# One hymba block on one core: borders of the first stage reordered, last chunk's q, k, v stores on GpSimd's queue, out-projection weights split in the first stage

## The chip, the cores and the metric

The kernel runs on 1 core of one Trainium2 chip. The metric is device time in microseconds (us) of one launch. TensorE is called PE here (its weight loads PEld), VectorE DVE, ScalarE ACT, GpSimd POOL or Pool, SyncE SP; those are the names that the profile uses.

## What is computed

One layer on a sequence of 2048 tokens of width 1024, fp32 in and out, cut to what matters here:

```
mod = silu(c) @ ada_w + ada_b                    # six vectors of 1024: shift, scale, gate, twice
h = rmsnorm(x) * (1 + scale1) + shift1
z = h @ w_in                                     # q, k, v (several branches), gates, zx, zy
o_nsa = compressed + selected + window attention, gated by sigmoid(zg)
   # compressed keys/values: gelu(blocks of 32 tokens @ cmp_w1) @ cmp_w2
o_lru = RG-LRU(zx) * gelu(zy)                    # conv of width 4, gates, a linear scan over the tokens
mixed = [rmsnorm(o_nsa) * nog, rmsnorm(o_lru) * log]
x = x + gate1 * (mixed @ w_out)
x = x + gate2 * conv_ffn(rmsnorm(x) * (1 + scale2) + shift2)
return rmsnorm(x) * final_norm_g
```

## The kernel before

Every matrix product that needs fp32 accuracy is three matmuls: both operands are split into a high part (`...h`, written by ACT as a copy in a shorter format) and a low part (`...l`, the difference, by DVE), and high x high, high x low and low x high are summed (L124, L125, `mm3` at L132).

The work has three stages, each with its tile pools. The first (0 to some 572 us of the trace) goes over four chunks of 512 tokens. A chunk is normalised (`norm_x`, L144 and L146: square, scale), transposed on PE and split (`norm_k`, L153 to L159: tiles `tp`, `hh`, `hl`), and then multiplied with tiles of 128 columns of `w_in`: `zc` (raw keys for compression, stored to C_d), `zx` (input of the RG-LRU), `zy`, `zq`, `zk`, `zv` with the gates. Weights come through `weights` in the order of the list `seq`: SP loads `wr`, ACT and DVE split it into `w..h`, `w..l`. q, k, v are split too and stored in DRAM (Q_d, K_d, V_d; buffers `st` x3 and `vst` x2). In the last chunk the compression's steps (`compress_load`, `compress_step`: load `xf` from C_d, split, multiply with `cmp_w1`) stand between the projections; the list TAIL gives the order of their weights.

Two side works run in the first stage. `ada_next` makes one more column block of `mod` at each call: SP loads `ad` (512 KB, one buffer: the next load waits until PE has used the one before), PE multiplies it (`aprb`, L174), and for the gate vectors SP also loads a row `ar` that DVE adds to and SP stores to G_d (L200 to L202). `wo_next` (chunks 1 and 2, in the loop over `zy`) multiplies 128 rows of `w_out` with the norms' gains and gate1 (DVE, L328) and stores the result to W_d as fp32.

The second stage ("t", attention, to about 1460 us) goes over 32 units of 128 tokens and one key group, beginning with tile 4: scores `sa` (compressed and window), minimum and exponential (`pc`), `ss` (selected blocks), transposed probabilities `pt` split into `th` (ACT) and `tl` (DVE), and `po`. `load_wo` (L630 to L637) loads W_d in this stage and splits it there into `wo`. The third stage is the FFN.

The order of instructions on each engine is not that of the code alone: a scheduler takes the code's order as a priority and each engine then runs its own list strictly in order, as does SP its DMA issues. So moving a call moves rows on all engines. What the change moves lies between about 40 and 700 us; from unit 4_1's successors on, and in the whole third stage, the order is as it was.

## Time and profile before

| | us |
|---|---|
| median of 3 runs | 2914.63 |
| lowest, highest | 2912.96, 2920.44 |
| profiled execution, its own time | 2917.85 |
| span in the trace (first to last instruction) | 2916.1 |

The profiled execution is 3.22 us above the median, and 1.75 us of it lie outside the span. Sums below are made against 2917.85 and then moved by -3.22 to the median. In the tables of stretches a line gives, for the stretch named first, its length and each engine's busy time with the number of instructions, then the mean granted clock of PE (1.00 is 2.4 GHz, 0.50 is 1.2 GHz), the share of the DMA engines and GB/s. In a timeline a line begins with its start and its duration; an idle time of the engine before it and what ended it stand in brackets.

### The profile page before, as it was taken

Reading aid. Unit: us, or ns where it says so; the run is one execution under the profiler, and the core shown is the slowest. Engines: PE = TensorE matmul, PEld = TensorE weight load, DVE = VectorE, ACT = ScalarE, POOL = GpSimd, SP = SyncE. Lnnn points to the kernel's source line nnn. Section 1 sums busy time; section 2 is a strip of 40 time slices with the busy share of each in tenths; the row PEclk is TensorE's granted clock in tenths of the full one; section 3 lists DMA queues with packets and bytes.
Section 4 is the critical chain, followed back from the end, with each engine's and each line's share of the span. In section 5 each row is a group of like instructions: output and inputs, shape, how many; then the busy total and the mean of one; then the engine's idle time right before and its main releaser. Section 6 shows DMA issues by size and latency. Waiting matters only on the chain.

```text
span 2916.1 us, 40471 instructions
## 1 busy us (share of the span) xinstructions
PE 2821.5 (97%) x14308; PEld 2324.5 (80%) x14308; DVE 1723.8 (59%) x3077; ACT 1484.6 (51%) x2686; POOL 1319.2 (45%) x1416
## 2 busy tenths in 40 slices
PE   8999999889999999999999999999999999999998
PEld 6777777767788777888788888888888888888887
DVE  4656656776777788888656621666216662266621
ACT  5656566577777677777643332433324333233322
POOL 1111010066666555555454445644455444555444
PEclk9999999989999999999999999999999999999999
DMA  7576765755544443443443333433334333343332
GB/s 287 178 271 201 244 210 141 208 162 138 145 124 127 121 128 104 115 120 105 153 139 94 100 118 101 152 96 100 122 97 152 99 94 123 101 138 94 97 99 80
DMA packets 262524, 399.47 MB, mean 137 GB/s; under 512 B 42033, under 2 KB 171057, under 8 KB 262321
## 3 DMA queue, kind: packets, MB, share of 16 engines
q1 hardware_dynamic: 261712, 395.70, 44.4%
q8 instruction: 114, 1.87, 0.3%
q0 software_dynamic: 320, 1.05, 0.1%
q14 instruction: 90, 0.73, 0.1%
q10 hardware_dynamic: 288, 0.13, 0.0%
HBM read 343.20 MB, written 53.61 MB: 136 GB/s over the span
## 4 chain that ended last, share of the span: by engine, by line
PE 80%; DVE 6%; ACT 5%; DMA 5%; issue 2%; POOL 1%; SPq 1%; POOLq 0%; DVEq 0%; ACTq 0%
PE pg L132 17%; PE pd L132 16%; PE pu L132 16%; PE p L132 6%; PE pt L786 5%; PE ss L647 3%; PE po L797 3%; PE po L798 3%; PE zy L132 2%; PE zx L132 2%; PE sa L647 2%; DMA xf<-C_d 1%; DVE tl L788 1%; PE zq L132 1%; ACT th L787 1%
## 5 line engine op out<-in xcount | busy, mean ns | idle before, releaser
L788 DVE TENSOR_TENSOR tl<-pt,th 128x512 fp32r<-128x512 f32 (+4 forms) x444 | 295.1, 683 | 47.6 <-ACT th L787 45.5
L945 DVE TENSOR_SCALAR ac<-gp,vec 128x512 f32<-128x512 f32 x88 | 191.5, 2176 | 201.5 <-ACT gp L942 198.8
L787 ACT ACTIVATE th<-pt 128x512 fp32r<-128x512 f32 (+4 forms) x444 | 254.7, 592 | 105.5 <-PE pt L786 100.8
L758 POOL TENSOR_SCALAR ps<-ps,rs,gates 128x1024 f32<-128x1024 f32 (+7 forms) x192 | 182.3, 959 | 163.2 <-DVE rs L755 118.8
L953 DVE TENSOR_TENSOR gl<-ac,gh 128x512 fp32r<-128x512 f32 x88 | 209.4, 2379 | 70.5 <-ACT gh L952 70.5
L978 DVE TENSOR_TENSOR y<-pd,g2b 128x512 f32<-128x512 f32 x32 | 21.9, 683 | 371.1 <-PE pd L132 371.1
L948 ACT ACTIVATE ac<-ac 128x512 f32<-128x512 f32 x88 | 55.6, 632 | 339.4 <-DVE ac L947 339.3
L752 ACT ACTIVATE ps<-ps,mn 128x1024 f32<-128x1024 f32 (+7 forms) x192 | 171.2, 895 | 52.3 <-DVE mn L652 51.9
L786 PE MATMUL pt<-ident,ps 128*128 128x128 f32 x1088 | 167.4, 275 | 6.0 <-DVE tl L788 5.2
L647 PE MATMUL ss<-ks,Q 128*128 128x512 f32 (+3 forms) x640 | 164.4, 379 | 4.2 <-DVE mn L652 2.9
L786 PEld LDWEIGHTS pt<-ident,ps 128*128 128x128 f32 x1088 | 133.1, 141 | 42.0 <-DVE tl L788 12.1
L647 PEld LDWEIGHTS ss<-ks,Q 128*128 128x128 f32 x640 | 116.2, 194 | 30.7 <-issue 4.8
L947 DVE SCALAR_TENSOR_TENSOR ac<-gp,vec,ac 128x512 f32<-128x512 f32 x176 | 134.3, 763 | 6.2
L798 PE MATMUL po<-tl,vs 128*128 128x512 f32 x272 | 123.6, 454 | 1.0 <-DVE tl L788 1.0
L797 PE MATMUL po<-th,vs 128*128 128x512 f32 x272 | 111.3, 409 | 6.4 <-ACT th L787 6.3
L652 DVE CUSTOM_DVE_ANT_1 ps<-ss,bi 128x1024 f32<-128x1024 f32 (+4 forms) x96 | 105.6, 1106 | 15.6 <-PE ss L647 10.3
L647 PE MATMUL sa<-K,Q 128*128 128x272 f32 (+14 forms) x464 | 99.1, 341 | 14.8 <-DVE mn L652 5.6
L786 PE MATMUL pt<-ident,pc 128*128 128x128 f32 (+9 forms) x688 | 103.7, 277 | 5.6 <-POOL pc L724 2.8
L726 POOL TENSOR_SCALAR pc<-pc,rs,gates 128x640 f32<-128x640 f32 (+4 forms) x128 | 104.2, 815 | 8.1 <-DVE mn L652 7.5
L401 POOL COPY hcar<-xc 128x1 f32<-128x1 f32 x16 | 19.4, 1212 | 180.7 <-DVE xc L400 180.0
L786 PEld LDWEIGHTS pt<-ident,pc 128*128 128x128 f32 (+9 forms) x688 | 81.7, 137 | 23.6 <-POOL pc L724 3.3
L949 DVE TENSOR_TENSOR ac<-ac,pu 128x512 f32<-128x512 f32 x88 | 60.5, 688 | 67.3 <-ACT ac L948 65.9
(1626 smaller groups left out, 8877.2 us busy)
## 6 DMA issues: line engine op xcount, KB each, us to landing
wg<-in_w_gu_dram SPq DMA_DIRECT2D x88, 512.0 KB, 3.6
wu<-in_w_gu_dram SPq DMA_DIRECT2D x88, 512.0 KB, 3.6
wd<-in_w_dn_dram SPq DMA_DIRECT2D x88, 512.0 KB, 3.6
wr<-in_w_in_dram SPq DMA_DIRECT2D x64, 512.0 KB, 5.5
ad<-in_ada_dram SPq DMA_DIRECT2D x32, 512.0 KB, 5.0
Q<-Q_d SPq DMA_DIRECT2D x64, 256.0 KB, 4.7
ks<-K_d SPq DMA_DIRECT2D x56, 256.0 KB, 3.4
vs<-V_d SPq DMA_DIRECT2D x56, 256.0 KB, 3.2
```

The costliest lines, as they stand in the source:

```text
L132: pe.matmul(ps, a, b, start=(n == 0), stop=(n == total - 1))
L647: pe.matmul(ps[:, o:o + W], Qt[:, hl, h * P:(h + 1) * P], K_ap, start=(hl == 0), stop=(hl == 1))
L752: act.activation(p, p, AF.Exp, scale=-1.0, bias=init, accum_out=sm[:, h, 2 + n:3 + n])
L758: pool.tensor_scalar(p, p, rs[:, h, 2:3], gt[:, h, 1:2], op0=OP.mult, op1=OP.mult)
L786: pe.transpose(pt[:, h * P:(h + 1) * P], jobs[n][0](h), ident)
L787: act.activation(th, pt, AF.Copy)
L788: dve.tensor_tensor(tl, pt, th.bitcast(F32), op=OP.subtract)
L797: pe.matmul(po, jobs[n][1], th, start=(n == 0), stop=False)
L798: pe.matmul(po, jobs[n][1], tl, start=False, stop=(n == N - 1))
L945: dve.tensor_scalar(ac, gp[:, 0:TC], V("fcw", f), V("fcb", f), op0=OP.mult, op1=OP.add)
L947: dve.scalar_tensor_tensor(ac, gp[:, k:k + TC], V("fcw", k * NF + f), ac, op0=OP.mult, op1=OP.add)
L953: dve.tensor_tensor(l, ac, h.bitcast(F32), op=OP.subtract)
```

## The change

- TAIL and `sequence`: in the last chunk the compression's steps and their weights begin after `zx3_1` and not after `zy3_0`; `compress_load(0)` comes right after `zc`. Then come the rest of q, then k, and v last.
- `norm_x` of the next chunk stands before the `zy` loop; it was before the q tiles.
- Two calls of `ada_next` move from the chunk's end to between q tiles. The sum of squares of the RG-LRU's output on PE (`pr`, L423) moves to the chunk's end (`lru_scale`).
- `wo_next` moves from the `zy` loop to the `zx` loop, takes its tiles from `st` instead of `x`, makes the split itself (ACT copy, DVE subtract) and stores both parts: W_d has twice the size. `load_wo` then loads 1 MB for each of 8 row blocks and splits nothing.
- In the last chunk all stores of q, k and v are issued from GpSimd's queue; before, only those of `qs3_3` were.

```diff
-TAIL = [("z", 4), ("c", 0), ("z", 5), ("c", 1), ("z", 6), ("c", 2), ("z", 7), ("c", 3), ("z", 8), ("c", 4), ("z", 9),
-        ("c", 5), ("z", 12), ("c", 6), ("z", 13), ("c", 7), ("v", 0), ("v", 1), ("z", 10), ("z", 11)]
+TAIL = [("z", 0), ("z", 1), ("c", 0), ("z", 2), ("c", 1), ("z", 3), ("c", 2), ("z", 4), ("c", 3), ("z", 5), ("c", 4),
+        ("z", 6), ("c", 5), ("z", 7), ("c", 6), ("z", 8), ("c", 7)] + [("z", j) for j in range(9, 14)] + [("v", 0), ("v", 1)]
...
-    W_d = dr.tile([KT, P, D], F32, name="W_d")
+    W_d = dr.tile([KT, P, 2, D], F32, name="W_d")
...
-            g1b = pl.tile([P, D], F32, name=f"g1b{k}", tag="x", bufs=4)
+            g1b = pl.tile([P, D], F32, name=f"g1b{k}", tag="st", bufs=3)
...
-            raw = pl.tile([P, D], F32, name=f"wor{k}", tag="x", bufs=4)
+            raw = pl.tile([P, D], F32, name=f"wor{k}", tag="st", bufs=3)
...
-            st = pl.tile([P, D], F32, name=f"wos{k}", tag="st", bufs=3)
-            dve.scalar_tensor_tensor(st, raw, gain, g1b, op0=OP.mult, op1=OP.mult)
-            sync.dma_start(W_d[k], st)
+            dve.scalar_tensor_tensor(raw, raw, gain, g1b, op0=OP.mult, op1=OP.mult)
+            h = pl.tile([P, D], F32R, name=f"wosh{k}", tag="st", bufs=3)
+            l = pl.tile([P, D], F32R, name=f"wosl{k}", tag="st", bufs=3)
+            act.activation(h, raw, AF.Copy)
+            dve.tensor_tensor(l, raw, h.bitcast(F32), op=OP.subtract)
+            sync.dma_start(W_d[k, :, 0, :], h.bitcast(F32))
+            sync.dma_start(W_d[k, :, 1, :], l.bitcast(F32))
...
+            if c + 1 == NCH:
+                compress_load(0)
...
                 ada_next()
-            if c + 1 == NCH:
-                compress_load(0)
+                if 0 < c < NCH - 1:
+                    wo_next()
+                if c + 1 == NCH and m > 0:
+                    compress_step(m - 1)
+            xs = norm_x(pl, x, c + 1, 4, ("t2", 2)) if c + 1 < NCH else None
             for m in range(4):
                 ps = z_tile(c, 4 + m, hT, f"zy{c}_{m}")
...
                 ada_next()
-                if 0 < c < NCH - 1:
-                    wo_next()
                 if c + 1 == NCH:
-                    compress_step(m)
+                    compress_step(m + 3)
...
+            def lru_scale():
                 pr = pp.tile([P, 4], F32, name=f"pr{c}", tag="g", bufs=2)
...
-                    (sync if c + 1 < NCH or j < 3 else pool).dma_start(
+                    (sync if c + 1 < NCH else pool).dma_start(
                         Q_d[h // 4, :, :, h % 4, t0:t0 + TC], st[hh * 64:(hh + 1) * 64].bitcast(F32))
...
-                    sync.dma_start(K_d[n, g, :, :, t0:t0 + TC].rearrange("l d t -> d l t"),
+                    (sync if c + 1 < NCH else pool).dma_start(K_d[n, g, :, :, t0:t0 + TC].rearrange("l d t -> d l t"),
...
-                    sync.dma_start(V_d[:, :, 4 * c + t].rearrange("n p g d -> p n (g d)"),
+                    (sync if c + 1 < NCH else pool).dma_start(V_d[:, :, 4 * c + t].rearrange("n p g d -> p n (g d)"),
...
             if c + 1 < NCH:
-                xs = norm_x(pl, x, c + 1, 4, ("t2", 2))
-                zs(range(8, 12))
+                zs((8, 9))
+                ada_next()
+                zs((10, 11))
+                ada_next()
                 lru_out()
...
                 v_tiles(lambda k: following(k + 3) if 1 <= k < 5 else None)
-                for _ in range(2):
-                    ada_next()
             else:
-                for n, j in enumerate((8, 9, 12, 13)):
-                    zs([j])
-                    compress_step(4 + n)
+                zs([8])
+                compress_step(7)
+                zs(range(9, 12))
                 lru_out()
+                zs((12, 13))
                 v_tiles()
-                zs((10, 11))
+            lru_scale()
             return nxt
...
-                raw = pl.tile([P, D], F32, name=f"wr{k}", tag="ps", bufs=10)
-                sync.dma_start(raw, W_d[k])
-                act.activation(t[:, 0], raw, AF.Copy)
-                dve.tensor_tensor(t[:, 1], raw, t[:, 0].bitcast(F32), op=OP.subtract)
+                sync.dma_start(t.bitcast(F32), W_d[k])
```

ACT at the start, where the last normalised parts of chunk 0 (`hh0_7`, `hl0_7`) are made, before:

```order
L176 ACTIVATE adrp7_573<-aprp7_556 128x256
L159 ACTIVATE hl0_6_536<-hf0_6_537,mod_78 128x512
L157 ACTIVATE hh0_7_585<-tp0_7_580,mod_78,A1_79 128x512
L176 ACTIVATE adrb16_683<-aprb16_674 128x128
L159 ACTIVATE hl0_7_586<-hf0_7_587,mod_78 128x512
L339 ACTIVATE cs0_0_647<-zf0_383 128x512
```

and in the changed kernel (`j1_..` and `x1_..` are the squares and scalings of chunk 1's tokens, `x1_0` to `x1_3`):

```order
L144 ACTIVATE j1_0_872,ss1_0_873<-x1_0_870 128x1024
L176 ACTIVATE adrp7_573<-aprp7_556 128x256
L144 ACTIVATE j1_1_881,ss1_1_882<-x1_1_879 128x1024
L159 ACTIVATE hl0_6_536<-hf0_6_537,mod_78 128x512
L146 ACTIVATE x1_0_870<-x1_0_870,rs1_0_875 128x1024
L144 ACTIVATE j1_2_890,ss1_2_891<-x1_2_888 128x1024
L157 ACTIVATE hh0_7_585<-tp0_7_580,mod_78,A1_79 128x512
L176 ACTIVATE adrb16_683<-aprb16_674 128x128
L146 ACTIVATE x1_1_879<-x1_1_879,rs1_1_884 128x1024
L144 ACTIVATE j1_3_899,ss1_3_900<-x1_3_897 128x1024
L146 ACTIVATE x1_2_888<-x1_2_888,rs1_2_893 128x1024
L159 ACTIVATE hl0_7_586<-hf0_7_587,mod_78 128x512
```

Both pieces begin behind `hh0_6`. Seven instructions of chunk 1's `norm_x` now stand between it and `hl0_7`.

SP at the border from chunk 2 to chunk 3 (`ad`: the next block of `ada_w`; `qs2_..`, `ls2_..`: stores of q and of the RG-LRU's output), before:

```order
L436 DMA Q_d_60<-qs2_1_3617 128x1x512 x2
L271 DMA wr54_3833<-in_w_in_dram 128x1024
L436 DMA Q_d_60<-qs2_2_3653 128x1x512 x2
L191 DMA ad42_3356<-in_ada_dram 128x1024
L202 DMA G2_d_82<-ar40_3313 128x128
L200 DMA ar41_3371<-in_rows_dram 128x128
L271 DMA wr55_3839<-in_w_in_dram 128x1024
L436 DMA Q_d_60<-qs2_3_3689 128x1x512 x2
L191 DMA ad43_3414<-in_ada_dram 128x1024
L417 DMA L_d_64<-ls2_0_3694 256x1x512
```

and in the changed kernel:

```order
L445 DMA Q_d_60<-qs2_1_3649 128x1x512 x2
L200 DMA ar41_3453<-in_rows_dram 128x128
L271 DMA wr54_3896<-in_w_in_dram 128x1024
L191 DMA ad43_3489<-in_ada_dram 128x1024
L445 DMA Q_d_60<-qs2_2_3704 128x1x512 x2
L202 DMA G2_d_82<-ar41_3453 128x128
L271 DMA wr55_3902<-in_w_in_dram 128x1024
L445 DMA Q_d_60<-qs2_3_3740 128x1x512
L200 DMA ar42_3504<-in_rows_dram 128x128
L445 DMA Q_d_60<-qs2_3_3740 128x1x512
L424 DMA L_d_64<-ls2_0_3764 256x1x512
```

`ad43` stands ahead of the stores of `qs2_2` and `qs2_3`; it stood behind them.

ACT at the end of the first stage (`vs3_..`: evacuation of v; `pc4_0`: the first exponentials of the attention stage), before:

```order
L463 ACTIVATE vs3_3_5301<-zv3_3_5189 128x4x64
L213 ACTIVATE get_5127<-get_5127 128x256
L432 ACTIVATE qs3_2_5331<-zq3_2_5306 128x512
L616 ACT_TABLE_LOAD
L616 ACTIVATE gates_86<-gates_86 128x384
L562 ACTIVATE VC_88<-vf_5139 128x2x64
L432 ACTIVATE qs3_3_5361<-zq3_3_5336 128x512
L699 ACT_TABLE_LOAD
L699 ACTIVATE pc4_0_5405,sm4_0_5407<-pc4_0_5405,mn4_0_5406 128x40
```

and in the changed kernel:

```order
L451 ACTIVATE ks3_0_5230<-zk3_0_5205 128x512
L572 ACTIVATE VC_88<-vf_5063 128x2x64
L451 ACTIVATE ks3_1_5266<-zk3_1_5241 128x512
L472 ACTIVATE vs3_0_5371<-zv3_0_5271 128x4x64
L472 ACTIVATE vs3_1_5376<-zv3_1_5272 128x4x64
L472 ACTIVATE vs3_2_5381<-zv3_2_5273 128x4x64
L472 ACTIVATE vs3_3_5386<-zv3_3_5274 128x4x64
L626 ACT_TABLE_LOAD
L626 ACTIVATE gates_86<-gates_86 128x384
L706 ACT_TABLE_LOAD
L706 ACTIVATE pc4_0_5437,sm4_0_5439<-pc4_0_5437,mn4_0_5438 128x40
```

The four `vs3` copies now stand directly ahead of the gates' sigmoid and the first exponentials, and the q copies ahead of them all. With two `vst` buffers `vs3_2` takes the buffer of `vs3_0`, whose store must have landed.

## Rows read from the trace of the kernel before

**Rows 1.** The page's first part: busy time, share of the span and instructions of each engine.

```profile
PE 2821.5 (97%) x14308; PEld 2324.5 (80%) x14308; DVE 1723.8 (59%) x3077; ACT 1484.6 (51%) x2686; POOL 1319.2 (45%) x1416
```

**Rows 2.** Table of stretches: three chunk borders, last chunk, start of attention, zx of chunk 1.

```profile
122.00:185.00 63.00, 55.19 (x371) 45.56 (x369) 32.95 (x52) 36.40 (x60) 9.21 (x13) 0.95 0.68 226
262.00:312.00 50.00, 45.50 (x325) 37.73 (x323) 25.63 (x44) 33.04 (x54) 7.90 (x11) 1.00 0.71 241
390.00:445.00 55.00, 48.92 (x324) 40.59 (x324) 25.03 (x44) 33.20 (x55) 7.37 (x12) 0.94 0.61 196
445.00:576.00 131.00, 120.90 (x662) 102.93 (x660) 97.50 (x158) 73.58 (x108) 12.07 (x21) 0.97 0.63 177
576.00:640.00 64.00, 52.33 (x251) 40.64 (x252) 49.50 (x181) 48.34 (x136) 32.02 (x58) 0.81 0.70 191
...
185.00:217.00 32.00, 32.00 (x152) 25.64 (x153) 26.06 (x36) 15.20 (x23) 6.80 (x8) 1.00 0.97 341
```

**Rows 3.** PE's waits from 0 to 700 us: us in total, times, longest.

```profile
PE aprb L174 <- DMA ad<-in_ada_dram: 9.8, 5, 3.7
...
PE aprb L174 <- ACT t L407: 5.6, 2, 2.8
PE sa L647 <- DMA K<-K_d: 4.6, 1, 4.6
...
PE sa L647 <- DMA Q<-Q_d: 2.8, 1, 2.8
...
PE pg L132 <- DVE ar L201: 2.4, 1, 2.4
```

**Rows 4.** ACT's timeline at border 0: norm_x among the evacuations.

```profile
143.01 1.04 ACT L144 ACTIVATE j<-x 128x1024 bf16<-128x1024 f32 x1
...
146.77 1.14 ACT L146 ACTIVATE x<-x,rs 128x1024 f32<-128x1024 f32 x1
```

**Rows 5.** ACT's timeline at the start: hl0_7.

```profile
54.17 0.72 ACT L159 ACTIVATE hl<-hf,mod 128x512 fp32r<-128x512 f32 x1 [0.65 <-DVE hf L158]
```

**Rows 6.** PE's timeline at the start: the first zx.

```profile
57.34 0.40 PE L132 MATMUL zx<-hh,w4h 128*128 128x512 f32 x1
```

**Rows 7.** SP's issues at border 0.

```profile
133.01 1.16 SPq L436 DMA_DIRECT2D Q_d<-qs  x2
134.28 0.57 SPq L191 DMA_DIRECT2D ad<-in_ada_dram  x1
```

**Rows 8.** DVE's timeline at border 0.

```profile
149.14 0.29 DVE L201 TENSOR_TENSOR ar<-ap,ar 128x128 f32<-128x128 f32 x1 [6.34 <-DMA ar<-in_rows_dram]
```

**Rows 9.** ACT and DVE on the tile wo alone, 576 to 640 us (stretches).

```profile
576.00:640.00 64.00, 0.00 (x0) 0.00 (x0) 9.72 (x8) 8.45 (x8) 0.81 0.70 191
```

**Rows 10.** PE's timeline: the last matmul of the first stage.

```profile
571.18 0.40 PE L132 MATMUL zq<-hh,w79l 128*128 128x512 f32 x1
```

**Rows 11.** ACT's timeline at the end of the first stage.

```profile
557.89 0.82 ACT L463 ACTIVATE vs<-zv 128x256 fp32r<-128x256 f32 x2
...
564.86 1.28 ACT L616 ACT_TABLE_LOAD   x1
566.15 0.53 ACT L616 ACTIVATE gates<-gates 128x384 f32<-128x384 f32 x1
...
579.26 0.33 ACT L699 ACTIVATE pc<-pc,mn 128x40 f32<-128x40 f32 x1
```

**Rows 12.** DMA issues, 545 to 600 us: KB each, median us to landing.

```profile
V_d<-vs SPq DMA_DIRECT2D x4, 256.0 KB, 2.4
...
Q_d<-qs POOLq DMA_DIRECT2D x2, 256.0 KB, 6.4
```

**Rows 13.** PE's timeline: two uses of ad in chunk 1, one after the other.

```profile
222.39 0.64 PE L174 MATMUL aprb<-ad,caz 128*32 128x128 f32 x16
...
234.06 0.65 PE L174 MATMUL aprb<-ad,caz 128*32 128x128 f32 x16
```

**Rows 14.** The page's list of DMA issues: count, KB each, median us to landing.

```profile
ad<-in_ada_dram SPq DMA_DIRECT2D x32, 512.0 KB, 5.0
```

More of the change, by code (lines that the diff above doesn't have):

```diff
@@ L252, in sequence @@
         def sequence(c):
-            head = [("z", 14), ("z", 15)] + [("z", j) for j in range(4)]
+            head = [("z", 14), ("z", 15)]
             if c < NCH - 1:
-                return head + [("z", 4 + j) for j in range(10)] + [("v", 0), ("v", 1)]
+                return head + [("z", j) for j in range(14)] + [("v", 0), ("v", 1)]
             return head + TAIL
```

## The prediction

> **What bounds the kernel now.** I read the busy shares first: PE works 97% of the span [rows 1], so time can only come from PE's idle time and from the stretches in which it runs at the lower of its two clocks. The change touches nothing behind some 700 us, so the table of stretches up to there says what can be won. In each stretch the time lost is the idle time (length less PE's busy time) plus the busy time times one less the mean granted clock: work at half clock takes twice as long, and a mean clock of 0.95 means a tenth of the time at 1.2 GHz, half of which is lost. From [rows 2]: border 0 to 1 (122 to 185 us) 7.8 + 55.2 x 0.05 = 10.6 us; border 1 to 2 (262 to 312) 4.5; border 2 to 3 (390 to 445) 6.1 + 48.9 x 0.06 = 9.0; last chunk (445 to 576) 10.1 + 120.9 x 0.03 = 13.7, of which 4.6 is the wait at its very end; start of attention (576 to 640) 11.7 + 52.3 x 0.19 = 21.6. That is 59 us. The table of PE's waits names the causes [rows 3]: the loads of `ad` (9.8), ACT's squares `t` ahead of `aprb` (5.6), the key load of the first unit (4.6), Q (2.8), DVE's `ar` ahead of `pg` (2.4).
>
> **The start: a loss of 5.** The first part of the change that PE meets is a cost. ACT runs its list in order, and four squares and three scalings of chunk 1 now stand ahead of `hl0_7`. A square takes 1.04 and a scaling 1.14 [rows 4], together 4 x 1.04 + 3 x 1.14 = 7.6 us; ACT's idle times there, 0.65 ahead of `hl0_7` [rows 5] and two like it before, take up about 1.7 of it (estimated). So `hl0_7` begins at about 60 and not at 54.2 [rows 5], and `zx` at about 63 and not at 57.3 [rows 6]. Eight transposes fill part of this gap and are gone from border 0. Loss about 5; 3 if ACT overlaps more, 8 if the x loads come late too or PE falls to half clock.
>
> **Border 0: a gain of 4.5 of 10.6.** Here `norm_x` no longer takes ACT (4 x 1.04 + 4 x 1.14 = 8.7 us) while k and v wait to be evacuated [rows 4], the transposes have their data early, and two steps of `ada_next` move from the end to between the q tiles, so that the single `ad` buffer is asked for at wider intervals. What the first wait was made of is in SP's queue: `ad` was issued at 134.28, right behind two stores of q that SP had held until q was ready [rows 7]. What I expect to remain is the chain of the gate row: DVE sits idle 6.34 us for `ar` [rows 8], which is loaded behind a store to G_d on SP, and everything that DVE evacuates stands behind it. I take under half of the loss; the ends are 0 and 10.6.
>
> **Borders 1 and 2: gains of 4 and 6.** At border 2 `ad43` now goes out ahead of the stores of `qs2_2` and `qs2_3`, as the order shows; the RG-LRU's chain ends earlier relative to PE's work, since `norm_x` is out of ACT's way, so both waits for `t` (2.8 each [rows 3]) should go at borders 1 and 2. Of 4.5 and 9.0 us I take 4 and 6. The ends are 0 and all of it.
>
> **Out-projection weights in the first stage: a loss of 2.** Eight products by DVE stay, and eight copies (ACT) and eight subtractions (DVE) move here from attention, where they take 8.45 and 9.72 us, 1.06 and 1.22 each [rows 9]. In the `zx` loop of a middle chunk DVE is busy 26.1 of 32 us [rows 2], and with 4 x 1.22 it is at 31 of 32: still hidden, barely. The DMA engines are busy 0.97 of that stretch already [rows 2]; with the `st` buffers shared by four uses the loads and stores spread over `zx`, `zy` and the first q tiles, and 2 MB more is written per chunk. Weight loads landed late there without PE noticing (no idle time in that stretch). I take 1 us per chunk, ends 0 and what the third rival gives.
>
> **The last chunk: a gain of 3.** Compression starts a few tiles earlier and its steps stand among the `zx` and `zy` tiles, so the RG-LRU's tail no longer meets its last steps on ACT and DVE. The wait for `ar` (2.4 [rows 3]) is the one wait that has a row; the rest is half clock; ends 0 and 6.
>
> **The end of the stage: a loss of 3 where the diff looks like a gain of 4.6.** The stores of q, k, v leave SP's queue, so the first unit's loads go out early and the key wait of 4.6 us [rows 3] disappears. But PE's first transposes wait for the exponentials, and these now stand behind v. Call T the end of PE's last first-stage matmul (before: 571.18 + 0.40 = 571.6 [rows 10]); the first exponential began at 579.26 [rows 11], T + 7.7. All four `zv` end close together, so `vs3_0` is evacuated and its store issued at about T. It must land before `vs3_2` can take its buffer. A q store on GpSimd's queue took 6.4 us to land, v stores on SP's 2.4 [rows 12], in a stretch less busy with loads. Taking 6.4, because queue and load are those of the changed kernel: `vs3_2` can begin at T + 6.4, `vs3_3` behind the second store at T + 7.1; then a copy (0.41), a table load (1.28), the gates' sigmoid (0.53) and another table load (1.28) [rows 11] put the first exponential at T + 10.6: 2.9 us later than before. Taking 2.4 it is T + 6.6, a gain of 1.1. If the four `wo` loads of 1 MB that now come at this moment slow the stores further, the loss may reach 6.
>
> The Trainium skill, page "DMA: Bandwidth & Descriptors", section "Issuing engine by pattern", says that plain stores belong to the hardware path of SyncE and that GpSimd's software path is generally slower, which speaks against this part. Its fit for one software DMA (section "Anatomy of one DMA — SWDGE (gpsimd) path"), 2.0 us plus bytes over 436,000 per us, would be an estimate of 2.6 us for 256 KB; the trace does not agree: its row has 6.4, and the sum goes by that. By 2.6 the first exponential would stand at T + 6.8 and the sum below would be 4 us lower.
>
> **The start of attention: a gain of 6.** From 576 to 640 us ACT and DVE split `wo` in the middle of the first units: 18.2 us of work of the two engines [rows 9], in a stretch where DVE is busy 49.5 and ACT 48.3 of 64 us [rows 2] and PE waits for `th` and `tl`. DVE's 9.7 us stood on the path for perhaps a third to a half of it. The wait for Q, 2.8 [rows 3], stood behind the loads of `wr` on SP and goes too: the first tile-0 unit that needs this Q comes after two units of tile 4. I take 6 of 21.6; ends 2 and 9.
>
> **Sum.** -5 + 4.5 + 4 + 6 - 2 + 3 - 3 + 6 = 13.5 us gained: 2917.85 - 13.5 = 2904.35 on the profiled execution, and 3.22 lower against the median: 2901.
>
> **Rivals.** *First, every wait goes:* the borders give all that they lose (10.6 + 4.5 + 9.0 in place of 14.5: 9.6 more), v stores land in 2.4 us (4 more), the start costs 3 (2 more). 2901 - 15.6 = 2885. For it: both engines have room at the borders (DVE 33 and ACT 36 of 63 us [rows 2]). Against it: the `ar` chain, which the change does not shorten.
>
> *Second, the waits move rather than go:* the borders give 7 and not 14.5, and of attention's gain only the Q wait, 2.8 and not 6. That is 10.7 less: 2912, no difference that can be told. For it: `ad` still has one buffer, the gate row is still a round trip through DRAM, and the start and the end of the stage both lose.
>
> *Third, slower: `ad` loads get stuck behind the stores of the split weights.* SP issues in order, and `ad` now stands behind stores that wait for ACT's copy or DVE's subtraction, in a stretch where DVE has 1 us of 32 to spare. Each late `ad` costs PE what it cost at the borders: 9.8 us in 5 waits, 2 each [rows 3], and again as much at half clock (border 2 shows 2.9 us of this beside 6.1 idle [rows 2]), so up to 4. The point at which it decides: two uses of `ad` lie 11.7 us apart in a middle chunk [rows 13] and a load takes 5.0 [rows 14], so SP must be held over 6 us. If that happens to seven of the some ten `ad` loads of chunks 1 and 2, it costs 7 x 4 = 28 us: 2901 + 28 = 2929. Against it: four pieces in about 60 us leave time to catch up.
>
> **How the numbers follow.** 0.3% (about 8.7 us) is what a measurement of this kernel can tell from no change: faster is below 2905.9, slower above 2923.4. My forecast, 2901 and between 2893 and 2906, has 0.44, the first rival (below 2893) 0.14, the second (2906 to 2923) 0.29, the third 0.13. So faster 0.58, same 0.29, slower 0.13. The range 2880 to 2924 leaves out the worst of the third and what lies below the first.
>
> **What would show it.** Right: in the changed trace PE waits some 5 us at about 55 to 62 for `hl`; no wait for K at the end of the stage but one of 10 us or more between `sa` and `pt`, with ACT idle ahead of `vs` for a DMA; at the borders fewer `aprb` waits; DVE without `wo` at 593 to 609. Wrong: `zx` or `zy` of chunks 1 and 2 with waits for `ad` or for `w..l` (third rival); PE waits for `ar` and `ad` at all three borders as long as before (second); the borders at full clock throughout (first).

## The result, and the profile after

The changed kernel takes 2889.94 us (median of 4 runs, 2889.51 to 2890.41); beside it the kernel before took 2914.28. The ratio is 0.9909 with a 95% interval of 0.9898 to 0.9921: 24.3 us less. The forecast was 2901 with a range of 2880 to 2924, so side and range held, but the gain is nearly twice the 13.5 us of the sum. Of the sum's eight terms the start and the cost of the split weights in the first stage come out near their size; the others do not.

The first part of the page and PE's waits up to 700 us of the changed kernel (waits: us in total, times, longest):

```profile
PE 2810.1 (97%) x14308; PEld 2319.6 (80%) x14308; DVE 1724.3 (60%) x3077; ACT 1486.2 (51%) x2686; POOL 1326.3 (46%) x1430
```

```profile
PE aprb L174 <- DMA ad<-in_ada_dram: 9.7, 6, 2.5
...
PE sa L654 <- DVE mn L659: 5.8, 3, 4.9
...
PE pt L793 <- POOL pc L731: 3.3, 1, 3.3
```

Against [rows 3]: the waits for K, for Q, for ACT's `t` and for `ar` are gone, and the sum of the waits for `ad` is as large as it was (9.7 beside 9.8). This sum hides a shift. At border 0 (130 to 170 us) the waits for `ad` fall from 6.6 to 2.8 us, as the prediction had it; at borders 1 and 2 they grow from 3.2 to 6.9 us, where the waits for `t` (5.6) are gone. PE's timeline at border 0 before, then after:

```profile
140.25 0.64 PE L174 MATMUL aprb<-ad,caz 128*32 128x128 f32 x16 [2.64 <-DMA ad<-in_ada_dram]
150.45 1.08 PE L174 MATMUL aprb<-ad,caz 128*32 128x128 f32 x16 [3.68 <-DMA ad<-in_ada_dram]
```

```profile
145.62 0.65 PE L174 MATMUL aprb<-ad,caz 128*32 128x128 f32 x16 [0.84 <-DMA ad<-in_ada_dram]
154.67 0.64 PE L174 MATMUL aprb<-ad,caz 128*32 128x128 f32 x16 [1.96 <-DMA ad<-in_ada_dram]
```

Where the time went is told by the start of the same piece of work in both traces (PE's timeline, us). The last column is the gain in a second trace of the changed kernel, `after_again`, which comes below as a control:

| start of | before | after | difference | gained since the line above | in the second trace |
|---|---|---|---|---|---|
| zx, chunk 0 | 57.3 | 63.9 | +6.6 | -6.6 | -5.9 |
| zk, chunk 0 | 123.5 | 129.6 | +6.1 | 0.5 | 0.9 |
| zq, chunk 1 | 229.8 | 228.3 | -1.5 | 7.6 | 5.2 |
| zk, chunk 1 | 256.4 | 255.0 | -1.4 | -0.1 | 0.0 |
| zq, chunk 2 | 357.3 | 355.0 | -2.3 | 0.9 | 1.5 |
| zk, chunk 2 | 384.0 | 381.6 | -2.4 | 0.1 | 0.0 |
| end of the last projection | 571.6 | 554.5 | -17.1 | 14.7 | 15.6 |
| first pt of attention | 586.3 | 570.1 | -16.2 | -0.9 | -0.5 |
| pt number 229 | 733.5 | 703.6 | -29.9 | 13.7 | 15.9 |

Behind that the difference stays within 1.7 us of -29.9 to the end (2916.1 and 2887.9 us of span). The two large entries are the last chunk with the border ahead of it, and the first units of attention. An entry of one trace is good to some 2 us only, as the last two columns show.

The same stretches by engine (PE, PEld, DVE, ACT, POOL busy; granted clock; DMA share; GB/s), first zk of chunk 2 to the end of the stage before, and then after:

```profile
384.00:571.60 187.60, 175.82 (x1011) 148.41 (x1009) 127.84 (x207) 107.80 (x163) 20.42 (x34) 0.96 0.61 181
```

```profile
381.60:554.50 172.90, 166.51 (x982) 143.15 (x980) 122.42 (x195) 98.53 (x148) 26.48 (x34) 0.99 0.67 198
```

By the reckoning of the prediction (idle time, plus busy time times one less the clock) 11.8 + 7.0 = 18.8 us were lost there and 6.4 + 1.7 = 8.1 are lost now. So of the 14.7 us gained 5.4 are idle time and 5.3 clock. The other 4.0 are work of PE that no longer lies in the stretch (982 matmuls and not 1011), one ada step of 16 matmuls and some transposes among it.

### The profile page after: what moved, and what is told of

It reads as the page before. It is cut to its first block, busy times and chain, and to the rows that moved or that the text cites. A ratio compares the mean times of both kernels' runs of the same rounds, so it can differ in the third digit from the quotient of the medians.

```text
span 2887.9 us, 40522 instructions
## 1 busy us (share of the span) xinstructions
PE 2810.1 (97%) x14308; PEld 2319.6 (80%) x14308; DVE 1724.3 (60%) x3077; ACT 1486.2 (51%) x2686; POOL 1326.3 (46%) x1430
## 4 chain that ended last, share of the span: by engine, by line
PE 85%; ACT 5%; DVE 5%; DMA 3%; issue 2%; POOL 1%; SPq 0%; POOLq 0%; ACTq 0%; DVEq 0%
PE pg L132 17%; PE pd L132 16%; PE pu L132 16%; PE p L132 6%; PE pt L793 5%; PE ss L654 4%; PE po L804 3%; PE po L805 3%; PE zx L132 3%; PE zy L132 3%; PE sa L654 2%; PE zq L132 1%; PE zc L132 1%; DVE tl L795 1%; DMA ad<-in_ada_dram 1%
## 5 line engine op out<-in xcount | busy, mean ns | idle before, releaser
L408 POOL COPY hcar<-xc 128x1 f32<-128x1 f32 x16 | 27.5, 1730 | 190.9 <-DVE xc L407 190.3
L659 DVE CUSTOM_DVE_ANT_1 ps<-ss,bi 128x1024 f32<-128x1024 f32 (+4 forms) x96 | 105.7, 1106 | 11.8 <-PE ss L654 6.5
L793 PE MATMUL pt<-ident,pc 128*128 128x128 f32 (+10 forms) x688 | 103.4, 276 | 5.7 <-POOL pc L731 3.3
L793 PEld LDWEIGHTS pt<-ident,pc 128*128 128x128 f32 (+10 forms) x688 | 81.4, 136 | 23.2 <-POOL pc L731 3.8
```

The costliest lines, as they stand in the source:

```text
L793: pe.transpose(pt[:, h * P:(h + 1) * P], jobs[n][0](h), ident)
```

## Experiments: the start and the first border

ACT at the start did what the order said it would. Of the changed kernel, ACT's timeline:

```profile
53.24 0.71 ACT L159 ACTIVATE hl<-hf,mod 128x512 fp32r<-128x512 f32 x1
53.86 1.15 ACT L146 ACTIVATE x<-x,rs 128x1024 f32<-128x1024 f32 x1
54.90 1.05 ACT L144 ACTIVATE j<-x 128x1024 bf16<-128x1024 f32 x1
...
59.88 0.72 ACT L159 ACTIVATE hl<-hf,mod 128x512 fp32r<-128x512 f32 x1
```

`hl0_7` begins at 59.88 (before 54.17 [rows 5]; forecast "about 60"). PE did not wait some 5 us for it in one piece, though. From 50 to 61 us it was idle for 3.1 us in five pauses, of which the longest was for a scaled `x` (PE's timeline):

```profile
60.04 0.44 PE L153 MATMUL tp<-ident,x 128*128 128x128 f32 x2 [1.64 <-ACT x L146]
```

Eight transposes of chunk 1 filled part of the rest, and from 57 to 64 us PE's mean granted clock was 0.81. Whether the early `norm_x` is a cost that could be had back was asked by two kernels. The first puts chunk 1's `norm_x` where it was:

```diff
-            xs = norm_x(pl, x, c + 1, 4, ("t2", 2)) if c + 1 < NCH else None
+            xs = norm_x(pl, x, c + 1, 4, ("t2", 2)) if 0 < c < NCH - 1 else None
...
             if c + 1 < NCH:
+                if xs is None:
+                    xs = norm_x(pl, x, c + 1, 4, ("t2", 2))
                 zs((8, 9))
```

> The changed kernel (2889.9 us), with norm_x of chunk 1 back ahead of the q tiles of chunk 0; chunks 1 and 2 keep the early norm_x. Theory 1: the early norm_x costs the 6.6 us by which the first zx came later, and border 0 gains its 5.5 us for other reasons (the ada steps between the q tiles): the start comes back to 57 us, border 0 keeps most of its gain, 2884 to 2886. Theory 2: border 0 gains because ACT is free of norm_x there, so what the start wins is given back: 2888 to 2891, zc of chunk 1 again at 161 to 163 us.

2895.87 us, ratio 0.9928 (0.9909 to 0.9947): as a time above the ranges of both theories, and only the trace decides between them. The first zx is back at 57.1 us, but zq of chunk 1 starts at 228.9, as in the changed kernel (228.3). PE's timeline at border 0 of this kernel shows the price back in its old place, in waits for `ad` as long as before (6.6 us from 130 to 170 us; these are the two long ones):

```profile
140.26 1.08 PE L174 MATMUL aprb<-ad,caz 128*32 128x128 f32 x16 [2.89 <-DMA ad<-in_ada_dram]
150.50 1.08 PE L174 MATMUL aprb<-ad,caz 128*32 128x128 f32 x16 [3.17 <-DMA ad<-in_ada_dram]
```

Theory 2 holds in the trace: what the start pays (6.6) is what border 0 saves. The two ada steps stand between the q tiles in this kernel too, so their wider spacing alone does not shorten these waits; `norm_x` off ACT does. That SP holds `ad` back behind stores of q that wait for ACT is what its order suggests [rows 7], and no run shows it by itself. The second kernel keeps the early call but gives the squares another scratch buffer, one that is in use until the zx loop ends, so that the scheduler cannot put them ahead of `hl0_7`:

```diff
-            xs = norm_x(pl, x, c + 1, 4, ("t2", 2)) if c + 1 < NCH else None
+            xs = norm_x(pl, x, c + 1, 4, ("t2" if c else "xp", 2)) if c + 1 < NCH else None
```

> The changed kernel (ratio 0.9909 to before), with the squares' scratch tiles of chunk 1's norm_x in the tag xp in place of t2, which is free only after the zx loop: norm_x of chunk 1 runs during the zy loop of chunk 0, not ahead of hl0_7 and not at border 0. Theory 1: the first zx comes back to 57 to 58 us and border 0 keeps what it gained, 5 to 7 us less than the changed kernel: ratio 0.9885 to 0.9893. Rival: ACT in the zy loop has no room for 8.7 us more beside its evacuations, and PE waits there or at border 0: 0.9905 to 0.992.

2884.64 us, ratio 0.9896 (0.9881 to 0.9911): the lowest median of all kernels here, just above theory 1's range and below the rival's. Its trace has zx at 56.9, zk of chunk 0 at 122.2, zq of chunk 1 at 222.9 and the end of the span 6.2 us ahead of the changed kernel's: theory 1. The eight operations now lie in the zy loop of chunk 0, where ACT waits for nothing more (groups of ACT from 57 to 122 us; busy, mean ns, idle before):

```profile
L146 ACT ACTIVATE x<-x,rs 128x1024 f32<-128x1024 f32 x4 | 4.6, 1142 | 0.0
L144 ACT ACTIVATE j<-x 128x1024 bf16<-128x1024 f32 x4 | 4.2, 1049 | 0.0
```

and PE, in the same stretch, has no idle time, where the changed kernel had 1.8 us (first this kernel's line, then the changed kernel's):

```profile
57.00:122.00 65.00, 65.00 (x337) 51.59 (x336) 42.28 (x62) 47.27 (x68) 9.02 (x16) 1.00 0.52 147
```

```profile
57.00:122.00 65.00, 63.19 (x319) 49.66 (x322) 39.57 (x58) 40.46 (x58) 3.08 (x10) 0.97 0.44 125
```

As a ratio it lies 1.3 thousandths below the first runs of the changed kernel and 2.6 below a second set of them on another chip, taken as a control:

> The changed kernel itself, beside the others on one chip: ratio 0.990 to 0.992 (0.9909 before).

2890.71 us, ratio 0.9922 (0.9909 to 0.9935). That is just above what was expected; the intervals of `k_xp` and of the two sets overlap by their ends, so its advantage of 4 to 8 us rests on the trace as much as on the ratios.

## Experiments: the borders and the last chunk

Two kernels take the kernel before and add one part each. One reorders the borders alone (early `norm_x`, ada steps between the q tiles, `lru_scale` at the end; `wo_next` in the zx loop because the early `norm_x` holds its buffers, but unsplit):

```diff
+            xs = norm_x(pl, x, c + 1, 4, ("t2", 2)) if c + 1 < NCH else None
             for m in range(4):
                 ps = z_tile(c, 4 + m, hT, f"zy{c}_{m}")
...
-                xs = norm_x(pl, x, c + 1, 4, ("t2", 2))
-                zs(range(8, 12))
+                zs((8, 9))
+                ada_next()
+                zs((10, 11))
+                ada_next()
...
-                for _ in range(2):
-                    ada_next()
...
```

> The kernel before, with the reordering of chunk borders alone: norm_x of the next chunk ahead of the zy loop, two ada steps between the q tiles, the RG-LRU's sum of squares at the chunk's end; wo_next moves to the zx loop (the early norm_x holds its buffers during the zy loop), but makes the unsplit product in the tag x as before. Theory 1 (the parts add up): the start loses 6.6, border 0 gains 5.5 to 7.5, border 1 some 3, border 2 its 5.8, and the last chunk, whose order is that of before, nothing: together 7 to 10 us, a ratio of 0.9966 to 0.9976. Rival: the gains of borders 1 and 2 need the rest of the change; no difference, 0.999 to 1.001.

2908.47 us, ratio 0.9976 (0.9964 to 0.9987): theory 1's time, but not its places. In the trace the last projection ends at 554.1 us, as in the changed kernel, and 12.4 of the 17.5 us gained by then come behind zk of chunk 2 (378.9 us), in border 2 and the last chunk, whose own order is that of before; theory 1 had 5.8 there. The profiled execution of this kernel is 4.7 us shorter than its median, that of the kernel before 3.6 longer than its own, so the trace shows the places better than the size: by the medians the whole gain is 6.9 us. The other kernel has the last chunk's order alone:

```diff
-TAIL = [("z", 4), ("c", 0), ("z", 5), ("c", 1), ("z", 6), ("c", 2), ("z", 7), ("c", 3), ("z", 8), ("c", 4), ("z", 9),
-        ("c", 5), ("z", 12), ("c", 6), ("z", 13), ("c", 7), ("v", 0), ("v", 1), ("z", 10), ("z", 11)]
+TAIL = [("z", 0), ("z", 1), ("c", 0), ("z", 2), ("c", 1), ("z", 3), ("c", 2), ("z", 4), ("c", 3), ("z", 5), ("c", 4),
+        ("z", 6), ("c", 5), ("z", 7), ("c", 6), ("z", 8), ("c", 7)] + [("z", j) for j in range(9, 14)] + [("v", 0), ("v", 1)]
...
-                for n, j in enumerate((8, 9, 12, 13)):
-                    zs([j])
-                    compress_step(4 + n)
+                zs([8])
+                compress_step(7)
+                zs(range(9, 12))
                 lru_out()
+                zs((12, 13))
                 v_tiles()
-                zs((10, 11))
```

> The kernel before, with the order of the last chunk alone: compression starts after zx3_1, v is last; all stores but those of qs3_3 stay on SP's queue. Theory 1: the last chunk gains the 9 to 12 us that it lost less in the changed kernel (waits for ar, for weights and for xf gone), the stage's end loses some of it since K and Q of the first unit are loaded behind the last stores: ratio 0.9965 to 0.9975. Rival: the last chunk's gain came from the borders before it (LRU and ada finished earlier), not from its own order: 0.999 to 1.001.

2930.1 us, ratio 1.0051 (1.0037 to 1.0064): slower. The last projection ends 4.5 us later than before, not earlier, and then PE waits for K (PE's waits; SP's timeline):

```profile
PE sa L650 <- DMA K<-K_d: 12.0, 1, 12.0
```

```profile
575.81 4.25 SPq L469 DMA_DIRECT2D V_d<-vs  x4
580.15 0.45 SPq L630 DMA_DIRECT2D MW<-in_mask_w_dram  x1
...
583.07 0.43 SPq L681 DMA_DIRECT2D K<-K_d  x1
```

So the last chunk's order gains nothing alone, most of the gain there belongs to the borders, and v last needs another queue. Behind the reordered borders the order may be worth some 2 us: from the first zk of chunk 2 to the end of the last projection `h_border_only` takes 175.2 us and `d_wo_old` (below), which has both orders and also splits in attention, 173.2 (before 187.6). That is no more than two traces of one kernel can differ by. Which step at the borders does it was asked by putting the two ada steps back:

```diff
-                zs((8, 9))
-                ada_next()
-                zs((10, 11))
-                ada_next()
+                zs(range(8, 12))
...
                 v_tiles(lambda k: following(k + 3) if 1 <= k < 5 else None)
+                for _ in range(2):
+                    ada_next()
```

> The changed kernel, with the two ada steps of each chunk back behind v_tiles. Theory 1: the 12 to 15 us that border 2 and the last chunk gained (also where only the borders were reordered) come in good part from the ada steps: back at the chunk's end, their loads are late again there and the last of them drag gate rows (ar) into the last chunk; 4 to 7 us of the gain go, ratio 0.992 to 0.9935. Rival: they come from norm_x, which no longer takes ACT at the border, and the ada steps are worth nothing: 0.990 to 0.9915.

2905.35 us, ratio 0.9971 (0.996 to 0.9982), further from the changed kernel than the 4 to 7 us of theory 1 (14.6 us by the medians of one chip). The last projection ends at 561.7 and not at 554.5 us; 5.3 of these 7.2 us come behind zk of chunk 2. Three waits are large here that are small or absent in the changed kernel (PE's waits):

```profile
PE zq L132 <- DVE w73l L125: 3.6, 1, 3.6
PE zv L132 <- DVE ks L452: 3.4, 2, 2.6
...
PE pg L132 <- DVE ar L201: 2.6, 1, 2.6
```

The first and the last lie in the last chunk, the second at the borders; the last is a wait of the kernel before [rows 3]. The waits for `ad` are the smallest of all kernels here (4.1 us in 2), so the two steps are not worth their own loads. What differs is that two of them now fall into the last chunk (`aprb` at 423.7 and 435.1 us; in the changed kernel there is none between 417.7 and 456.2). From 405 to 505 us, the end of border 2 and most of the last chunk, DVE waits longer for the compression's loads `xf`. For the gate rows it waits longer in the changed kernel (DVE's waits, this kernel and then the changed one):

```profile
DVE xf L536 <- DMA xf<-C_d: 15.8, 9, 4.8
```

```profile
DVE xf L537 <- DMA xf<-C_d: 9.9, 9, 2.2
DVE ar L201 <- DMA ar<-in_rows_dram: 8.3, 2, 5.6
```

The `ar` for which `pg` waits was itself held by such an `xf`: DVE had been idle 4.83 us for it. That the steps' loads and stores on SP are what delays `xf` is argued from this, not shown. The 7.2 us are half of the 14.6; the other half it loses later, mostly behind 600 us of the trace, and no line shows where.

## Experiments: the end of the stage and GpSimd's queue

The prediction took 6.4 us for a v store on GpSimd's queue. In the changed kernel ACT waited like this, its first two `vs` freed by the stores that GpSimd issued at 554.51 (POOL's timeline, then ACT's):

```profile
554.51 1.46 POOL L475 DMA_DIRECT2D V_d<-vs  x2 [9.49 <-DVE gates L474]
```

```profile
553.37 0.77 ACT L472 ACTIVATE vs<-zv 128x256 fp32r<-128x256 f32 x2 [10.55 <-PE zv L132]
557.40 0.38 ACT L472 ACTIVATE vs<-zv 128x256 fp32r<-128x256 f32 x1 [3.26 <-DMA V_d<-vs]
559.55 0.38 ACT L472 ACTIVATE vs<-zv 128x256 fp32r<-128x256 f32 x1 [1.77 <-DMA V_d<-vs]
...
563.09 0.33 ACT L706 ACTIVATE pc<-pc,mn 128x40 f32<-128x40 f32 x1
```

The first store had landed 2.9 us after its issue. The mechanism is as forecast, each `vs` behind a store, but the first exponential stands at T + 8.6 and not at T + 10.6 (T = 554.5; before T + 7.7), a loss of 0.9. The fit cited in the prediction (the Trainium skill, "DMA: Bandwidth & Descriptors", section "Anatomy of one DMA — SWDGE (gpsimd) path"), 2.6 us for 256 KB, agrees with this first store and not with the last two, which landed beside full DMA engines (busy share 1.12 from 558.5 to 567.5 us; 4 MB of `wo` loads were issued from 561.9 on) and took 6.7 us (DMA issues from 556 to 575 us):

```profile
wo<-W_d SPq DMA_DIRECT2D x4, 1024.0 KB, 10.8
...
V_d<-vs POOLq DMA_DIRECT2D x2, 256.0 KB, 6.7
```

What the queue is worth was measured by putting the stores back on SP in the changed kernel:

```diff
-                    (sync if c + 1 < NCH else pool).dma_start(
+                    (sync if c + 1 < NCH or j < 3 else pool).dma_start(
...
-                    (sync if c + 1 < NCH else pool).dma_start(K_d[n, g, :, :, t0:t0 + TC].rearrange("l d t -> d l t"),
+                    sync.dma_start(K_d[n, g, :, :, t0:t0 + TC].rearrange("l d t -> d l t"),
...
-                    (sync if c + 1 < NCH else pool).dma_start(V_d[:, :, 4 * c + t].rearrange("n p g d -> p n (g d)"),
+                    sync.dma_start(V_d[:, :, 4 * c + t].rearrange("n p g d -> p n (g d)"),
```

> The changed kernel, with the last chunk's stores of q, k and v on SP's queue as before (qs3_3 stays on GpSimd's). Theory 1: with v last, the first unit's loads of Q and K stand behind the last stores of v on SP, as in the kernel that had only the new order of the last chunk, where PE waited 12.0 us for K: 6 to 8 us slower than the changed kernel, ratio 0.993 to 0.994. Rival: the scheduler puts the loads ahead of the stores, PE waits for the exponentials as now, and the time is that of the changed kernel: 0.990 to 0.9915.

2897.49 us, ratio 0.9944 (0.9931 to 0.9957), 6.8 us above the changed kernel on the same chip: theory 1, at its price. PE's timeline:

```profile
570.81 4.84 PE L654 MATMUL sa<-K,Q 128*128 128x340 f32 x16 [12.07 <-DMA K<-K_d]
```

Two kernels take ACT's wait for the stores away by giving `vs3_2` and `vs3_3` other buffers: the tag `hf`, and then one buffer of `st`.

```diff
-                    st = pl.tile([P, 4, 2, DH], F32R, name=f"vs{c}_{t}", tag="vst", bufs=2)
+                    st = pl.tile([P, 4, 2, DH], F32R, name=f"vs{c}_{t}", tag="hf" if c + 1 == NCH and t > 1 else "vst", bufs=2)
```

> The changed kernel, with vs3_2 and vs3_3 in the two buffers of the tag hf, which is idle in the last chunk, so that they wait for no store to land. Theory 1: the first exponential comes 5.0 us earlier (the 3.26 and 1.77 us for which ACT waited for the stores), the first pt some 4 to 5 us earlier, 2885 to 2886. Rival: something else is late next at that place (the scores' minima on DVE, the table loads, the loads of K and of the masks), and the time stays within 1 us of 2889.9.

2894.05 us, ratio 0.9914 (0.9899 to 0.9928): no difference. ACT copied all four at once, but DVE's first scores then waited for stores of v, which fits that their tile lies in the memory of `hf` (DVE's timeline):

```profile
566.04 0.20 DVE L659 CUSTOM_DVE_ANT_0 pc<-sa,ci 128x40 f32<-128x40 f32 x1 [7.67 <-DMA V_d<-vs]
```

```diff
+                    if c + 1 == NCH and t > 1:
+                        if t == 2:
+                            both = pl.tile([P, 2, 4, 2, DH], F32R, name="vs23", tag="st", bufs=3)
+                        st = both[:, t - 2]
...
```

> The changed kernel, with vs3_2 and vs3_3 together in one buffer of the tag st, whose memory is not that of the first scores (the buffers of hf are, and there the scores had to wait until the last store of v had landed). Theory 1: ACT no longer waits for the stores of vs3_0 and vs3_1 (3.3 and 1.8 us) and nothing takes their place: the first pt comes 4 to 5 us earlier after the last projection, at 11 us behind it and not 15.5; ratio 0.9890 to 0.9898. Rival: the loads of K, Q and the masks for the first unit or the tables are late next: the first pt still 14 to 16 us behind, ratio 0.9905 to 0.992.

2895.13 us, ratio 0.9929 (0.9917 to 0.9942). The first pt came 10.5 us after the last projection (568.7 and 558.2) and not 15.6, as theory 1 had it. Yet the kernel is no faster, its ratio lies above the rival's range too: PE ran into the next wait, at the first scores of the third unit (tile 0).

```profile
603.63 0.88 PE L659 MATMUL sa<-K,Q 128*128 128x136 f32 x3 [6.27 <-DMA vs<-V_d]
```

The line names a load of v, but what landed just before was this unit's Q, issued on SP from 592.76 us on (DMA issues from 592.5 to 593.9 us):

```profile
Q<-Q_d SPq DMA_DIRECT2D x2, 256.0 KB, 9.9
```

Between 569 and 591 us the DMA engines were full:

```profile
569.00:591.00 22.00, 20.00 (x106) 15.50 (x106) 18.72 (x63) 15.40 (x38) 12.82 (x23) 0.88 1.04 393
```

The 8 MB of `wo` (issued from 565.9 to 584.0 us) are what is moved there, with loads of the second unit, and the third unit's Q is issued behind them on SP. The last kernel has the edits of `k_xp` and `b2_vs_in_st` and also puts the first four `wo` loads ahead:

```diff
             sync.dma_start(Kt[:, C:W].bitcast(F32),
                            K_d[1, g, :, :, (i + 1 - nw) * P:(i + 1) * P].rearrange("l d t -> (l d) t"))
+            if (i, g) == (TILES[0], 0):
+                load_wo(range(4, 8))
             Ks = []
...
-                    load_wo(range(4 - 4 * n, 8 - 4 * n))
+                    if n:
+                        load_wo(range(0, 4))
```

> The changed kernel with three edits: norm_x of chunk 1 in the zy loop (scratch in tag xp), vs3_2 and vs3_3 in one st buffer, and the first four wo loads (4 MB) issued right behind the first unit's K. Theory 1: with vs3 in st the end of the stage was 5.1 us shorter, but PE then waited 6.3 us in the second unit for loads behind 8 MB of wo; with half of these loads ahead, this wait goes and both gains stay: 9 to 11 us less than the changed kernel, ratio 0.987 to 0.988. Rival: the 8 MB are the bound of the first 35 us of attention whatever their order, and only norm_x's gain stays: 0.989 to 0.990.

2892.8 us, ratio 0.9927 (0.9912 to 0.9942), with runs from 2886.03 to 2899.01: worse than `k_xp` alone. The first pt is again 10.5 us behind the last projection, then `ss` waits 3.4 us for `ks`, which now stands behind `wo`, and PE runs 36 us at a low mean clock:

```profile
562.20:597.80 35.60, 29.54 (x122) 21.97 (x122) 19.77 (x68) 16.76 (x41) 14.31 (x25) 0.69 1.00 306
```

Neither theory is shown by this: the DMA share of 1.00 speaks for the rival, but 306 GB/s is less than the 393 reached above. Whether the 5 us at the end of the stage can be kept with the `wo` loads spread further is open; it wasn't tried.

## Experiments: the split of the out-projection weights

Once undone in the changed kernel, once alone in the kernel before:

```diff
-                sync.dma_start(t.bitcast(F32), W_d[k])
+                raw = pl.tile([P, D], F32, name=f"wr{k}", tag="ps", bufs=10)
+                sync.dma_start(raw, W_d[k])
+                act.activation(t[:, 0], raw, AF.Copy)
+                dve.tensor_tensor(t[:, 1], raw, t[:, 0].bitcast(F32), op=OP.subtract)
...
```

> The changed kernel, with the out-projection weights stored unsplit again and split in attention as before (the product with the gains stays in the zx loop, in buffers of the tag x). Theory 1: the 13.5 us that PE gained between the first pt and 750 us come from the split, which stood on the path of ACT and DVE: 2901 to 2904. Rival: only a part comes from it (the 2.8 us wait for Q and a third of 9.7 us of DVE, 6 us, as predicted), the rest from the earlier loads and stores: 2895 to 2897.

2902.71 us, ratio 0.9946 (0.9931 to 0.9961), 10.8 us above the changed kernel by the ratios. Its trace has the last projection's end at 552.2 us, 2.3 earlier than the changed kernel: that is what the split costs the first stage (forecast 2). The cost shows in chunk 2: from zk of chunk 1 to zq of chunk 2 this kernel takes 96.3 us, the changed one 100.0 and the kernel before 100.9. So border 1 gains 4.6 us where the split is not in the way, and 0.9 where it is. Between the first pt and pt number 229 it gains nothing on the kernel before (18.9 and 19.1 us ahead), where the changed kernel gains 13.7, and a wait of PE for Q (3.3 us) is there as before: all of that is the split, theory 1. The same transpositions (numbers 28 to 97), before, undone, and changed:

```profile
599.30:639.10 39.80, 31.85 (x164) 24.16 (x163) 32.81 (x119) 33.30 (x99) 21.04 (x39) 0.87 0.57 143
```

```profile
583.00:620.40 37.40, 29.26 (x149) 21.94 (x147) 29.83 (x111) 29.26 (x85) 21.22 (x42) 0.86 0.58 134
```

```profile
584.40:608.60 24.20, 22.57 (x141) 17.75 (x140) 20.05 (x85) 19.47 (x62) 15.77 (x31) 1.00 0.93 237
```

With the split in attention PE was idle 8.0 of 39.8 us and lost 31.85 x 0.13 = 4.1 more to the clock; without it 1.6 of 24.2, at full clock. Some of the difference of 15.6 us is other matmuls that moved out of the stretch (164 and 141). Over these transpositions the mean granted clock is 0.86 or 0.87 in all four kernels that split in attention, and 1.00 in eight of the ten traces without it (0.90 and 0.95 in `b2_vs_in_st` and `p_k_st_early`).

> The kernel before (2914.3 us), with the split of the out-projection weights alone moved into the first stage (zx loop, tag st). Theory 1: attention gains 12 to 13 us and the first stage loses at most 2: 2902 to 2904. Rival (that of the prediction): ad loads and weights come late behind the stores of the split parts, PE waits in zx and zy of chunks 1 and 2, and half of the gain or more is lost: 2908 or above.

2911.76 us, ratio 0.9979 (0.997 to 0.9988): in the rival's range. Attention gains 13.0 us (6.9 us behind at the first pt, 6.1 ahead at pt number 229), but the first stage ends 7.8 us later than before. The waits for `ad` have grown from 9.8 us in 5 to (PE's waits, 57 to 600 us)

```profile
PE aprb L174 <- DMA ad<-in_ada_dram: 11.5, 7, 2.9
...
PE zq L132 <- DVE w70l L125: 2.3, 1, 2.3
PE zx L132 <- ACT w21h L124: 1.7, 1, 1.7
```

while those for `t` are gone. Of the 7.8 us 5.3 lie between zk of chunk 1 and zq of chunk 2 (106.2 us, before 100.9), where PE's mean granted clock was 0.97 and not 1.00, and where PE waited for `ad` in the zx loop, at a place without such a wait before (PE's timeline):

```profile
296.24 1.08 PE L174 MATMUL aprb<-ad,caz 128*32 128x128 f32 x16 [2.51 <-DMA ad<-in_ada_dram]
```

So `ad` comes late, as in the prediction's third rival, but this one not for the reason it gave: SP had issued it at 290.17, behind a row of `w_out` (289.08) and two stores of v, and the first stores of split parts in chunk 2 come after it (298.63). The cost is real where the ada steps stand as before, and much smaller (2.3 us) in the changed kernel, which spaces them otherwise.

## Why the prediction was right, and where its sizes were off

- **The start, -5.** Right in place and near in size: 6.6 measured (5.9 in the second trace), `hl0_7` at 59.88 as forecast. The wait of some 5 us for `hl` did not come in one piece; 3.1 us of pauses, the transposes and a mean clock of 0.81 stood in its place. What the prediction didn't see is that this was a price only of where the scheduler put it (`k_xp`).
- **Border 0 and the weights of chunk 1, 4.5 - 1.** 7.6 measured, 5.2 in the second trace, for the reason given first (`norm_x` off ACT), as `a_start_late` shows; PE sees it as shorter waits for `ad` (2.8 us and not 6.6). The wider intervals of the ada steps, given beside it, are not the reason.
- **Border 1 and chunk 2, 4 - 1.** 0.9 measured; the wait for `t` went and a wait for `ad` came. The 4 for the border was right where the split is not in the way (4.6 in `d_wo_old`). The mis-sized term is the 1 for the split in chunk 2, which is 3.7.
- **Border 2 and the last chunk, 6 + 3.** 14.7 measured. The step that failed is the attribution: the last chunk's own order was to give 3 and gives less than nothing alone (-2.5 in `f_tail_only`) and perhaps 2 behind the reordered borders, while the borders' order alone gives 12.4 there (`h_border_only`) and not 6. The ada steps, weighed only as a matter of wider intervals for one buffer, give 5.3 of it (`n_ada_back`).
- **The end, -3.** The mechanism came as told, at -0.9; PE's pause ahead of the first pt is 8.2 us in two parts (4.9 and 3.3) and not one of 10. The mis-sized term is the 6.4 us: the first store took 2.9. Without GpSimd's queue PE would have waited 12.07 us for K (`c2_qkv_on_sp`), not 4.6, since v is now last; that the queue mends what the new order breaks wasn't in the sum.
- **Attention, 6.** 13.7 measured, all of it from the split (`d_wo_old`). Mis-sized: of 18.2 us of ACT and DVE work the sum let a third to a half of DVE's part count, and nothing for the clock, which was 0.87 there and is 1.00 now.
- **The rivals.** The first came nearest in time (2885), with one part of its mechanism, the short first v store; the start cost more and not less, and waits for `ad` stayed at every border. The third's late `ad` appears in `e_wo_only`, once at least without the stores that it named ahead of it.

Against the table of starts, border 0, the last chunk and attention were put too low by 4.1, 5.7 and 7.7 us, the end by 2.1; the start and border 1 too high by 1.6 and 2.1. With small entries between them that makes 29.9 us by pt number 229 instead of 13.5; 28.2 are left at the end of the span. The medians differ by 24.3 only, since the profiled execution of the kernel before lies 3.6 us above its median beside the changed kernel and that of the changed kernel 0.3 below its own. The range held because it was wide, not because the terms were near.

## What to carry to other kernels

A call that is moved earlier to free an engine at one border may be put by a scheduler into the first gap that its buffers allow, ahead of something that is waited for; a scratch buffer that comes free at the right moment holds it back. Look behind the name that a wait gives: the `ar` that held `pg` in `n_ada_back` was itself held by a load of another kind, and where an ada step stands decided what DVE waited for in the next chunk, not how long its own load took. Work on helper engines in a stretch where PE pauses can cost twice, as idle time and as clock (8.0 and 4.1 of 39.8 us here); count both. Take a second trace of the same kernel before reading an entry of 2 us out of one.

## What the runs showed of the hardware that was not expected

A 256 KB store on GpSimd's queue landed in 2.9 us with the DMA engines at a busy share of 0.53 (554.5 to 557.4 us of `after`) and in 6.7 us at 1.12 (558.5 to 567.5 us). In attention's first units (transpositions 28 to 97) PE's mean granted clock was 0.86 to 0.87 in the four kernels with the split among the evacuations and 1.00 in eight of ten traces without.
